# The opening of a transformer layer: where buffers lie, when late tiles are transposed, and where bias tables are written

## The chip, the cores and the metric

The kernel runs on one core of a Trainium2 chip. A core has a matrix engine (TensorE, PE in the profile), a vector engine (VectorE, DVE), a scalar engine (ScalarE, ACT), a general engine (GpSimd, POOL) and a queue engine (SyncE, SP). Each runs its own list of instructions in order and waits at semaphores for the others. DMA transfers are issued from the lists of SP, ACT and POOL. TensorE reads from the on-chip memory SBUF and writes to the accumulation memory PSUM, which has eight banks. The metric is the device time of one execution in microseconds (us). An execution's own time is slightly longer than the span of its instructions.

## The reference: one encoder layer

The input x has 1024 tokens of 1024 numbers. Everything is float32.

```
h = swiglu(rmsnorm(x, ffn1_pre_g), w_gate, w_up, w_down)       # 1024 -> 2816 -> 1024
x = x + 0.5 * rmsnorm(h, ffn1_post_g)
qkv = rmsnorm(x, mix_pre_g) @ w_qkv                            # 16 heads of 64
o_na  = neighbourhood_attention(q, k, v of heads 0..7,  na_rel_bias)
o_dil = dilated_mixture_attention(q, k, v of heads 8..15, t5_rel_bias)
x = x + rmsnorm(concat(rmsnorm(o_na), rmsnorm(o_dil)) @ w_out, mix_post_g)
h = swiglu(rmsnorm(x, ffn2_pre_g), ...)                        # second FFN
x = x + 0.5 * rmsnorm(h, ffn2_post_g)
```

`rmsnorm(x, g)` is `x / sqrt(mean(x*x) + 1e-6) * g`, and `swiglu(x)` is `(silu(x @ w_gate) * (x @ w_up)) @ w_down`. The dilated heads add a bias that depends on the distance of two tokens: a table of 511 values a head, looked up from `t5_rel_bias`.

## The kernel before, in words

**Arithmetic.** A float32 product is made from three faster ones. Each operand is split into a rounded part hi (a cast on ACT) and the rest lo (a subtraction on DVE), and `mm3` (lines 315 to 317) adds hi*hi, hi*lo and lo*hi in PSUM. The large products use Strassen's scheme (in Winograd's form) on 2 x 2 blocks: seven block products, of operands A11, S2, S1, S4, A12, S3 and A22 with weights B11, T2, T1, B22, B21, T3 and T4. For the tokens, tiles 0 to 3 (of 128 tokens each) are the upper half and tiles 4 to 7 the lower half; the sums S1 to S4 need both.

**The first FFN's opening.** `layer` writes the order of the head out by hand (lines 1436 to 1548): there PE, DVE and ACT follow the program's order, afterwards only PE does, and a scheduler places the other engines' instructions. Input tiles x0 to x3 are loaded, squared and summed (`square`, a pass on ACT, or on DVE for half a tile), scaled by the reciprocal root and the gain (`scaled`, line 1480), transposed on TensorE (line 157) and split (lines 164 and 165) into the columns of A11 and A12. A copy of every transposed half (line 236) goes to DRAM (line 237), where the later half tiles find it again. The gain row is spread over the partitions by a matmul (line 302) and copied in two halves (line 303).

**Turns.** `PairGemm.ahead` works through the first nine blocks (`early` = 9) of gate and up weights: a block is A11 (12 matmuls) times the gate weights and, one step later (`late`), A12 times the same weights. After each block a planned turn runs: `F` queues squares and scaling of two late tiles (4 to 7), `L` loads two tiles, `U` puts the two transposes of one late tile behind the next matmuls (`put`, `one`, `left_half`, `right_half`; DVE lines 264 to 274). Each group of matmuls calls `c.step()` twice, which runs one queued sum and one queued transpose. `ready`, before the ninth block, empties these queues, closes the pool `xp` and opens the pool of the full weight blocks; its two 8 KB (per partition) buffers `wraw` are loaded on SP (`fetch`, lines 405 and 406). `begin` then makes the weight sums of block 0 (lines 500 to 502) and splits them (lines 411 and 412), each behind the last DVE or ACT instruction issued so far. Only then `run` can start with S2.

**Memory.** Pools are stacked from the two ends of SBUF; `xp` and the pool that follows it lie at the right end. Inside a pool each tag has its own place, in the order in which the tags are first used. A tile waits for all readers of older tiles that lie on its place. The tags of `xp` are x (4 buffers of 4 KB), xn (3 of 4 KB), pre (the gain, 4 KB), s and x1.

**Runs over 22 blocks.** `run` (line 525 on) does the five remaining products of each early block in 60 matmuls; each block's sums are made one block ahead, and a weight buffer is loaded again as soon as its last split is done. The q,k projection later uses the same class with 8 blocks, all early, and writes q and k to DRAM from POOL (lines 928 to 934).

**Bias tables.** `bias_steps` (line 810 on) prepares the attention's tables on POOL's queue during the first FFN's `run`. `table(i)` makes two tables of 8 x 511 values (matmul on line 834) and `toeplitz(i, q)` (line 843) copies one of them from DRAM to DRAM into 32 shifted rows a head of `gab`, 511 KB each, eight copies in all, in turns 5 to 8. The first attention head reads `gab` (line 1005) when q,k's turn 5 has come.

Of the kernel before, what the change touches and what calls it, by code (L numbers as in the profile page):

```python
# [19 lines left out]
P, T = 128, 512  # L20
# [148 lines left out]
class Operand:  # L169
# [51 lines left out]
    def one(self, t, later=None):  # L221
# [6 lines left out]
        if t < 4:  # L228
            if t not in self.raw:
                two = c.xp.tile([P, 2, 2, 4, P], F32, tag="s", name="raw", bufs=c.deep)  # L230
                self.raw[t], self.raw[t + 1] = two[:, 0], two[:, 1]
            raw, i = self.raw[t], 0 if b == A11 else 1
            ps = transpose_in(c, src, *[h[:, :, cols] for h in self.x[b]])

            def keep():
                c.nc.scalar.copy(raw[:, i], ps)
# [55 lines left out]
def spread_gain(c, g, tag, row, one):  # L292

    nc = c.nc
    t = c.xp.tile([P, D], F32, tag=tag, name="gain", bufs=1)
    nc.gpsimd.memset(one, 1.0)
    nc.sync.dma_start(row, g)
# [92 lines left out]
class PairGemm:  # L390
# [4 lines left out]
    def __init__(self, c, op, srcs, early, sink):  # L395
        self.c, self.op, self.srcs, self.early, self.sink = c, op, srcs, early, sink
        self.n, self.raw, self.w, self.kept, self.own = len(srcs), {}, {}, {}, None
# [17 lines left out]
    def mm(self, ps, w, i, a, go_on=False, cols=slice(0, T)):  # L415
        hi, lo = w
        xhi, xlo = self.op.x[a]
        for k in range(4):
# [32 lines left out]
    def ahead(self, begun=(), ready=None):  # L451
# [358 lines left out]
def bias_steps(c, rel, t5, onehot, lncount, cmask):  # L810
# [420 lines left out]
def layer(tc, a, out):  # L1231
    nc = tc.nc
    c = Ctx(tc)
    with ExitStack() as ctx:
# [77 lines left out]
        def ffn(which, op, prep, pg, get, turns, sums, more, post, pre, src, dst, begin=None, tables=()):  # L1312
# [7 lines left out]
            if begin:  # L1320
                left_pool(e)
                pg.start()
# [113 lines left out]
        with ExitStack() as order:  # L1436
# [9 lines left out]
            half = [slice(0, T), slice(T, D)]  # L1446
            xs = {t: c.xp.tile([P, D], F32, tag="x", name="x", bufs=4) for t in range(4)}
            xn = [c.xp.tile([P, D], F32, tag="xn", name="xn", bufs=c.xn) for _ in range(2)] + [xs[2], xs[3]]
            op0 = Operand(c, None, 0)
            op0.gain, *gains = spread_gain(c, a["ffn1_pre_g"], "pre", xn[0][:1], xn[1][:1, :P])  # L1450
            for t in range(2):
                for h, q in enumerate((nc.sync, nc.scalar)):
                    q.dma_start(xs[t][:, half[h]], x0[t][:, half[h]])

            def begin(pg):
# [7 lines left out]
                def junk():  # L1463
                    return c.xp.tile([P, D], F32, tag="s", name="junk", bufs=2)
# [75 lines left out]
                for b in range(3):  # L1540
                    if b:
# [3 lines left out]
                    (lo0, lo1, lo2)[b](1)  # L1545
                order.close()
# [5 lines left out]
                                    {0: [F(4, 5), L(6, 7)], 3: [F(6, 7), U(4)], 4: [U(5)], 6: [U(6)], 7: [U(7)]},  # L1552
# [60 lines left out]
            plan(8, {5: [lambda: queued(load_head)], 7: [lambda: queued(load_head), lambda: queued(first_bias),  # L1613
# [204 lines left out]
```

## Time and profile before

| | us |
|---|---|
| median of 3 runs (lowest, highest) | 1928.7 (1925.5, 1930.73) |
| the profiled execution's own time | 1927.12 |
| its span, first to last instruction | 1925.3 |
| PE busy | 1850.6 (96%) |
| DVE busy | 1328.0 (69%) |
| ACT busy | 832.9 (43%) |
| POOL busy | 321.4 (17%) |

A line of the timeline gives the start in us, the duration in us, the engine, the line of the kernel, the operation with output and input, their shape, the count, and in brackets how long the engine had been idle and whose result ended the idle time. SPq, ACTq and POOLq are the queues in which DMA transfers are issued. A busy PE is not necessarily a PE at full speed: the stretches also give the granted clock.

### The profile page before, as it was taken

Reading aid. Unit: us, or ns where it says so; the run is one execution under the profiler, and the core shown is the slowest. Engines: PE = TensorE matmul, PEld = TensorE weight load, DVE = VectorE, ACT = ScalarE, POOL = GpSimd, SP = SyncE. Lnnn points to the kernel's source line nnn. Section 1 sums busy time; section 2 is a strip of 40 time slices with the busy share of each in tenths; the row PEclk is TensorE's granted clock in tenths of the full one; section 3 lists DMA queues with packets and bytes.
Section 4 is the critical chain, followed back from the end, with each engine's and each line's share of the span. In section 5 each row is a group of like instructions: output and inputs, shape, how many; then the busy total and the mean of one; then the engine's idle time right before and its main releaser. Section 6 shows DMA issues by size and latency. Waiting matters only on the chain.

```text
span 1925.3 us, 25132 instructions
## 1 busy us (share of the span) xinstructions
PE 1850.6 (96%) x8904; PEld 1535.5 (80%) x8904; DVE 1328.0 (69%) x2233; ACT 832.9 (43%) x1491; POOL 321.4 (17%) x504
## 2 busy tenths in 40 slices
PE   7899999999999999999999998998999999999997
PEld 5687787888878878788799997776888888888886
DVE  5877767766565878658577765678788777654557
ACT  6522233333443547323588765455222333344332
POOL 2123211110112013122423100021111111110000
PEclk9899999999999999999999999999999999999999
DMA  7646556653987767746877431475456655476663
GB/s 257 216 155 214 181 208 237 239 210 124 329 315 235 256 209 261 252 129 225 292 234 246 166 135 59 150 278 192 158 192 239 214 194 208 159 263 223 197 230 134
DMA packets 169008, 404.95 MB, mean 210 GB/s; under 512 B 17761, under 2 KB 40193, under 8 KB 166834
## 3 DMA queue, kind: packets, MB, share of 16 engines
q1 hardware_dynamic: 121042, 242.66, 37.7%
q0 software_dynamic: 46832, 158.59, 22.7%
q10 hardware_dynamic: 1008, 2.10, 0.3%
q8 instruction: 70, 1.15, 0.2%
q14 instruction: 56, 0.46, 0.1%
HBM read 277.34 MB, written 130.99 MB: 212 GB/s over the span
## 4 chain that ended last, share of the span: by engine, by line
PE 72%; DVE 9%; DMA 8%; issue 5%; ACT 4%; POOL 1%; SPq 0%; DVEq 0%; POOLq 0%; ACTq 0%
PE mmp L315 14%; PE mmp L317 14%; PE mmp L316 14%; PE accp L316 7%; PE accp L317 7%; PE accp L315 7%; DMA wraw<-in_wu_dram 3%; PE po L1064 2%; PE ptp L974 2%; PE po L1176 2%; DMA tsv<-tr 1%; PE sp L1043 1%; DVE pw L672 1%; DVE wlo L412 1%; PE sp L1160 1%
## 5 line engine op out<-in xcount | busy, mean ns | idle before, releaser
L315 PE MATMUL mmp<-x,whi 128*128 128x512 f32 (+1 forms) x1464 | 582.0, 398 | 28.5 <-ACT whi L411 11.9
L317 PE MATMUL mmp<-x,wlo 128*128 128x512 f32 (+1 forms) x1464 | 578.0, 395 | 1.2 <-DVE wlo L412 1.2
L316 PE MATMUL mmp<-x,whi 128*128 128x512 f32 (+1 forms) x1464 | 576.5, 394 | 0.8 <-DVE x L165 0.7
L315 PEld LDWEIGHTS mmp<-x,whi 128*128 128x128 f32 x1464 | 278.6, 190 | 93.9 <-ACT whi L411 17.5
L317 PEld LDWEIGHTS mmp<-x,wlo 128*128 128x128 f32 x1464 | 278.2, 190 | 66.5 <-DVE wlo L412 3.8
L316 PEld LDWEIGHTS mmp<-x,whi 128*128 128x128 f32 x1464 | 278.7, 190 | 62.0 <-DVE x L165 1.6
L672 DVE TENSOR_TENSOR pw<-praw,pw 128x1024 fp32r<-128x1024 f32 (+1 forms) x181 | 203.1, 1164 | 117.5 <-ACT pw L671 116.5
L671 ACT CAST pw<-praw 128x1024 fp32r<-128x1024 f32 (+1 forms) x181 | 168.8, 982 | 211.4 <-PE accp L317 151.9
L411 ACT CAST whi<-wraw 128x1024 fp32r<-128x1024 f32 x129 | 135.6, 1051 | 247.4 <-PE mmp L316 216.7
L316 PE MATMUL accp<-pw 128*128 128x512 f32 x600 | 234.0, 390 | 4.3 <-DVE pw L672 4.1
L315 PE MATMUL accp<-pw 128*128 128x512 f32 x600 | 234.5, 391 | 0.0
L317 PE MATMUL accp<-pw 128*128 128x512 f32 x600 | 233.6, 389 | 0.0
L412 DVE TENSOR_TENSOR wlo<-wraw,whi 128x1024 fp32r<-128x1024 f32 x129 | 158.3, 1228 | 27.0 <-ACT whi L411 26.9
L316 PEld LDWEIGHTS accp<-pw 128*128 128x128 f32 x600 | 112.7, 188 | 29.4 <-DVE pw L672 6.2
L315 PEld LDWEIGHTS accp<-pw 128*128 128x128 f32 x600 | 112.6, 188 | 23.9 <-ACT pw L671 0.3
L317 PEld LDWEIGHTS accp<-pw 128*128 128x128 f32 x600 | 112.6, 188 | 23.2
L619 POOL DMA_DIRECT2D g<-sg x44 | 23.9, 544 | 442.8 <-DVE sg L612 252.8
L411 ACT CAST whi<-traw 128x512 fp32r<-128x512 f32 x52 | 32.3, 622 | 148.4 <-DVE traw L501 92.6
L573 DVE TENSOR_TENSOR c<-mmp,u 128x512 f32<-128x512 f32 x52 | 35.8, 689 | 76.2 <-PE mmp L317 76.2
L430 ACT COPY s<-mmp 128x512 f32<-128x512 f32 x52 | 30.5, 587 | 129.5 <-PE mmp L317 117.2
L500 DVE TENSOR_TENSOR wraw<-wraw 128x1024 f32<-128x1024 f32 x52 | 63.6, 1223 | 32.1 <-DMA wraw<-in_wu_dram 26.2
L383 DVE TENSOR_TENSOR tr<-tr 128x1024 f32<-128x1024 f32 x26 | 31.7, 1219 | 39.4 <-DMA tr<-in_wd_dram 22.0
(275 smaller groups left out, 2774.4 us busy)
## 6 DMA issues: line engine op xcount, KB each, us to landing
praw<-g SPq DMA_DIRECT2D x70, 512.0 KB, 5.4
wraw<-in_wg_dram SPq DMA_DIRECT2D x44, 512.0 KB, 4.1
wraw<-in_wu_dram SPq DMA_DIRECT2D x44, 512.0 KB, 6.6
tr<-in_wd_dram SPq DMA_DIRECT2D x44, 512.0 KB, 6.5
g<-sg POOLq DMA_DIRECT2D x88, 256.0 KB, 3.5
ts<-tr POOLq DMA_DIRECT2D x22, 1024.0 KB, 4.7
praw<-ts SPq DMA_DIRECT2D x88, 256.0 KB, 4.3
praw<-in_wd_dram SPq DMA_DIRECT2D x66, 256.0 KB, 5.1
```

The lines of the kernel that those rows point to most:

```text
L315: nc.tensor.matmul(out, ahi, bhi, start=start, stop=False, skip_group_check=go_on)
L316: nc.tensor.matmul(out, ahi, blo, start=False, stop=False, skip_group_check=go_on)
L317: nc.tensor.matmul(out, alo, bhi, start=False, stop=stop, skip_group_check=go_on)
L411: nc.scalar.copy(hi, raw)
L412: nc.vector.tensor_sub(lo, raw, hi.bitcast(F32))
L500: nc.vector.tensor_sub(r[:, 0:2], r[:, 1:3], r[:, 0:2])
L573: nc.vector.tensor_add(c21, d, u2)
L671: nc.scalar.copy(hi, raw[:, :m])
L672: nc.vector.tensor_sub(lo, raw[:, :m], hi.bitcast(F32))
L974: nc.tensor.transpose(ps[:, j, :], src[:, j * P:(j + 1) * P], c.ident)
L1064: nc.tensor.matmul(po[:, un * 2 + j], pt[:, 2 * j + t, :], rhs, start=t == 0, stop=t == 1)
L1176: nc.tensor.matmul(po[0][:, u], pt[0][:, j, :], vs[:, k0 + j, :], start=j == 0, stop=j == n - 1)
```

## The change

Five things are changed.

1. `xp`'s tags are first used in the order s, x1, xn, pre, x. The third weight block (`w2`) lies in a buffer of x1 instead of xn, and the gain's tile is made by the caller of `spread_gain`.
2. In the head, the first two weight blocks are loaded in halves, the first halves ahead of x2 and x3 in the program, the second halves behind. The copies of the gain move behind squares, and the copies of the transposed tiles 2 and 3 (`keeps`) behind the last 6 matmuls of block 1's first group, which in turn move behind these tiles' transposes.
3. For the inline case of `one` (tiles 0 to 3), ACT makes the cast and the copy at once, and DVE subtracts from the copy in SBUF instead of from PSUM.
4. `ready` comes one block sooner in the first FFN (`before` = 2), and the late tiles' steps `U` two turns sooner (one for `F(6, 7)`).
5. The eight `toeplitz` copies move from the first FFN to turns 0 to 3 of the q,k run, two a turn, each behind POOL's last instruction.

```diff
@@ Operand.one
-            ps = transpose_in(c, src, *[h[:, :, cols] for h in self.x[b]])
+            hi, lo = [h[:, :, cols] for h in self.x[b]]
 
             def keep():
                 c.nc.scalar.copy(raw[:, i], ps)
                 c.nc.gpsimd.dma_start(self.saved[t][:, i], raw[:, i].rearrange("p k x -> p (k x)"))
-            keep() if later is None else later.append(keep)
+            if later is None:
+                ps = transposed(c, src)
+                c.nc.scalar.copy(hi, ps)
+                keep()
+                c.nc.vector.tensor_sub(lo, raw[:, i], hi.bitcast(F32))
+            else:
+                ps = transpose_in(c, src, hi, lo)
+                later.append(keep)
@@ PairGemm.ahead
-            if ready and b == self.early - 1:
+            if ready and b == self.early - self.before:
                 ready()
@@ bias_steps
-        for q in range(4):
-            step(5 + 2 * i + q // 2, toeplitz, i, q)
...
+    c.toeplitz = [lambda i=i, q=q: c.behind(lambda: toeplitz(i, q), POOL) for i in range(2) for q in range(4)]
@@ layer, head
+            first_junk = [c.xp.tile([P, D], F32, tag="s", name="junk", bufs=2)]
+            w2 = c.xp.tile([P, D], F32, tag="x1", name="w2", bufs=2)
+            xn = [c.xp.tile([P, D], F32, tag="xn", name="xn", bufs=c.xn) for _ in range(2)]
+            gain = c.xp.tile([P, D], F32, tag="pre", name="gain", bufs=1)
             xs = {t: c.xp.tile([P, D], F32, tag="x", name="x", bufs=4) for t in range(4)}
...
             def begin(pg):
+                for b in range(2):
+                    pg.raw[b] = c.wg.tile([P, 2, T], F32, tag="g", name="graw")
+                pg.raw[2] = w2.rearrange("p (i x) -> p i x", i=2)
+                for b in range(2):
+                    nc.sync.dma_start(pg.raw[b][:, 0], pg.srcs[b][0][:, half[0]])
                 nc.scalar.dma_start(xs[2], x0[2])
                 nc.sync.dma_start(xs[3], x0[3])
-                w2 = c.xp.tile([P, D], F32, tag="xn", name="w2", bufs=c.xn)
-                pg.raw[2] = w2.rearrange("p (i x) -> p i x", i=2)
+                for b in range(2):
+                    nc.sync.dma_start(pg.raw[b][:, 1], pg.srcs[b][0][:, half[1]])
                 nc.sync.dma_start(w2, pg.srcs[2][0])
...
                 square(0)
-                gains[0]()
                 square(1, 0)
                 square(1, 1, xn[1][:, half[1]])
+                gains[0]()
...
-                for f in keeps:
-                    f()
+                while keeps:
+                    keeps.pop(0)()
                 acc, s1 = [pg.bank() for _ in range(3)], []
-                for b in range(2):
-                    pg.mm(acc[b], pg.w[b], 0, A11, cols=slice(0, 256))
+                pg.mm(acc[0], pg.w[0], 0, A11, cols=slice(0, 256))
+                pg.mm(acc[1], pg.w[1], 0, A11, cols=slice(0, 256), ks=range(2))
                 r1 = next(root)
                 scaled(r1, 0, 2, 3)
-                op0.one(2)
-                op0.one(3)
+                op0.one(2, keeps)
+                op0.one(3, keeps)
+                pg.mm(acc[1], pg.w[1], 0, A11, cols=slice(0, 256), ks=range(2, 4))
+                while keeps:
+                    keeps.pop(0)()
...
+                pg.before = 2
...
-                                    {0: [F(4, 5), L(6, 7)], 3: [F(6, 7), U(4)], 4: [U(5)], 6: [U(6)], 7: [U(7)]},
+                                    {0: [F(4, 5), L(6, 7)], 1: [U(4)], 2: [F(6, 7), U(5)], 4: [U(6)], 5: [U(7)]},
@@ layer, q,k run
-            plan(8, {5: [lambda: queued(load_head)], 7: [lambda: queued(load_head), lambda: queued(first_bias),
+            plan(8, {**{i: c.toeplitz[2 * i:2 * i + 2] for i in range(4)}, 5: [lambda: queued(load_head)], 7: [lambda: queued(load_head), lambda: queued(first_bias),
```

More of the change, by code (lines that the diff above doesn't have):

```diff
@@ L289, in rstd_by_sqrt, with spread_gain @@
     yield y
-def spread_gain(c, g, tag, row, one):
+def spread_gain(c, t, row, one):
     nc = c.nc
-    t = c.xp.tile([P, D], F32, tag=tag, name="gain", bufs=1)
-    nc.gpsimd.memset(one, 1.0)
-    nc.sync.dma_start(row, g)
     copies = []
@@ L413, in split, with mm @@
         return hi, lo
-    def mm(self, ps, w, i, a, go_on=False, cols=slice(0, T)):
+    def mm(self, ps, w, i, a, go_on=False, cols=slice(0, T), ks=range(4)):
         hi, lo = w
         xhi, xlo = self.op.x[a]
-        for k in range(4):
+        for k in ks:
             sl = slice(k * P, (k + 1) * P)
@@ L1446, in layer @@
             half = [slice(0, T), slice(T, D)]
+            first_junk = [c.xp.tile([P, D], F32, tag="s", name="junk", bufs=2)]
+            w2 = c.xp.tile([P, D], F32, tag="x1", name="w2", bufs=2)
+            xn = [c.xp.tile([P, D], F32, tag="xn", name="xn", bufs=c.xn) for _ in range(2)]
+            gain = c.xp.tile([P, D], F32, tag="pre", name="gain", bufs=1)
             xs = {t: c.xp.tile([P, D], F32, tag="x", name="x", bufs=4) for t in range(4)}
-            xn = [c.xp.tile([P, D], F32, tag="xn", name="xn", bufs=c.xn) for _ in range(2)] + [xs[2], xs[3]]
+            xn += [xs[2], xs[3]]
             op0 = Operand(c, None, 0)
-            op0.gain, *gains = spread_gain(c, a["ffn1_pre_g"], "pre", xn[0][:1], xn[1][:1, :P])
+            nc.gpsimd.memset(xn[1][:1, :P], 1.0)
             for t in range(2):
@@ L1463, in junk @@
                 def junk():
-                    return c.xp.tile([P, D], F32, tag="s", name="junk", bufs=2)
+                    return first_junk.pop() if first_junk else c.xp.tile([P, D], F32, tag="s", name="junk", bufs=2)
                 def square(t, h=None, to=None):
```

6 lines of the change are left out of this document (4 added, 2 removed).

## The prediction

> **What bounds the kernel now.** I read the page first: the span, and the chain of work that ended last.
>
> ```profile
> span 1925.3 us, 25132 instructions
> ...
> PE 72%; DVE 9%; DMA 8%; issue 5%; ACT 4%; POOL 1%; SPq 0%; DVEq 0%; POOLq 0%; ACTq 0%
> ```
>
> TensorE carries 72% of the chain; what can be won is its idle time. Next, busy time by stretch (PE, PEld, DVE, ACT, POOL, then granted clock, DMA share, GB/s), for the first FFN's opening:
>
> ```profile
> 60.00:80.00 20.00, 20.00 (x96) 16.29 (x95) 19.14 (x28) 13.82 (x24) 4.33 (x8) 1.00 0.35 128
> 80.00:100.00 20.00, 11.56 (x37) 8.46 (x36) 11.11 (x14) 3.73 (x5) 0.54 (x1) 0.74 0.81 288
> ```
>
> PE is full until 80, then half idle at a clock of 0.74. The PE timeline (start, duration, and in brackets the idle time before) gives the places:
>
> ```profile
> 21.16 0.38 PE L315 MATMUL mmp<-x,whi 128*128 128x256 f32 x1 [2.07 <-ACT x L164]
> 21.89 0.39 PE L316 MATMUL mmp<-x,whi 128*128 128x256 f32 x1 [0.34 <-DVE x L165]
> ...
> 33.04 0.49 PE L315 MATMUL mmp<-x,whi 128*128 128x512 f32 x1 [2.32 <-ACT x L164]
> 33.88 0.50 PE L316 MATMUL mmp<-x,whi 128*128 128x512 f32 x1 [0.34 <-DVE x L165]
> ...
> 80.65 0.39 PE L317 MATMUL mmp<-x,wlo 128*128 128x512 f32 x1
> 89.11 0.80 PE L315 MATMUL mmp<-x,whi 128*128 128x512 f32 x1 [8.07 <-ACT whi L411]
> ...
> 90.70 0.80 PE L317 MATMUL mmp<-x,wlo 128*128 128x512 f32 x1 [0.37 <-DVE wlo L412]
> ...
> 95.56 0.57 PE L316 MATMUL mmp<-x,whi 128*128 128x512 f32 x1
> 95.97 0.40 PE L317 MATMUL mmp<-x,wlo 128*128 128x512 f32 x1
> ```
>
> A 512-column matmul starts every 0.233 us when TensorE is warm (80.65 is followed by nothing, so its slot ends at 80.88). Between 80.88 and 95.97 only 14 matmuls start, worth 3.3 us: 11.8 us are lost, 8.4 idle and 3.4 to the slow clock. This gap is the largest single loss of the kernel. What ends it, in the queue waits, the SP and the DVE timelines:
>
> ```profile
> SPq L405 <- DVE x L264: 23.9, 1, 23.9
> ...
> 80.33 0.65 SPq L405 DMA_DIRECT2D wraw<-in_wg_dram  x1
> ...
> 60.49 2.47 DVE L206 SCALAR_TENSOR_TENSOR xn<-x,y,gain 128x1024 f32<-128x1024 f32 x2
> ...
> 86.24 1.22 DVE L500 TENSOR_TENSOR wraw<-wraw 128x1024 f32<-128x1024 f32 x1 [5.93 <-DMA wraw<-in_wu_dram]
> ```
>
> SP stood 23.9 us before the first full weight load, until the last DVE split of a late tile (L264): the load's buffer lies on memory that these splits read. The input rows themselves are dead after L206, at 63.
>
> **The change, part by part.** *Buffers and the earlier ready step.* The xp tags are now made in the order s, x1, xn, pre, x. Before, the load waited for readers of s and x1, the last tags made; so the last tag lies where the next pool begins, and that is now x (4 x 4 KB, as large as the two 8 KB weight buffers). The load then waits for L206, at 63 or sooner. The ready step runs one turn sooner (24 matmuls, 5.6 us), and SP's remaining early loads are out by 56.2. So the load of 5.9 us (80.33 to 86.24) lies under matmuls. What is late next is DVE: L500, the two subtractions behind it and two splits, 86.24 to 90.65, 4.4 us, put behind the split of the ninth block and before the last 12 matmuls. I leave 0.8 us of gap: gain 11.0. Bounds: 4 (ready data, but the chain from 86.24 to 89.11 and part of the clock loss stay) to 11.8.
>
> *Head.* Rows of ACT, DVE and POOL:
>
> ```profile
> 6.50 0.58 ACT L303 COPY gain<-gps 128x512 f32<-128x512 f32 x1 [1.03 <-PE gps L302]
> 6.98 0.63 ACT L150 ACTIVATE junk<-x 128x512 f32<-128x512 f32 x1
> ...
> 7.74 0.16 DVE L281 TENSOR_TENSOR v<-ss 128x2 f32<-128x2 f32 x1 [1.76 <-ACT junk L150]
> ...
> 9.23 1.41 DVE L1480 SCALAR_TENSOR_TENSOR xn<-x,y,gain 128x512 f32<-128x512 f32 x2
> ...
> 20.03 0.58 ACT L236 COPY raw<-trp 128x512 f32<-128x512 f32 x1 [0.76 <-DVE x L165]
> ...
> 23.39 1.20 POOL L1444 DMA_DIRECT2D x<-in_x_dram  x2
> ...
> 28.39 1.06 ACT L150 ACTIVATE xn<-x 128x1024 f32<-128x1024 f32 x1 [0.99 <-DMA x<-in_x_dram]
> ```
>
> The square of tile 1 stood behind the gain copy, which waited 1.03 for its matmul. Now it fills that wait: DVE starts at 6.3 instead of 7.74, ACT's root follows the copy at 7.0, the first scaling comes at 8.1 instead of 9.23: 1.1 us. SP now loads the first halves of two weight blocks, then x3, then their second halves and the third block, which go to casts after the first scaling; its two more issues, 0.36 each like the others, stand ahead only of these late halves. The third block's buffer is now one of x1's two; tile 5's saved half needs it only at that tile's second transpose, so I charge nothing (without that cover, one 5 us load). At 21.16 the two casts L164 were parted by the copy L236, which waited for DVE. Kept for later, both go back to back, and 6 of the 24 narrow matmuls (0.12 us each) wait behind the transposes as cover: L316 starts near 18.5, not 21.89, so 3.4 us are won to there, the 1.1 among them. The stall at 33.04 had ACT waiting for tile 4's rows (28.39) ahead of the last casts. Their load, 23.39, follows the scaling of tiles 0 and 1 and moves by the same 3.4; so this stall may stay whole (gain 3.4), or go with its 2.7 idle and some 1.7 of slow clock (7.8). L236 no longer waits for DVE, which speaks for the upper half; the scheduler, free to put the squares before the casts, for the lower. I take 6.
>
> *Late tiles two turns sooner.*
>
> ```profile
> 35.51 1.28 DVE L206 SCALAR_TENSOR_TENSOR xn<-x,y,gain 128x1024 f32<-128x1024 f32 x1
> ...
> 48.01 0.60 PE L157 MATMUL trp<-ident,xn 128*128 128x128 f32 x4
> ...
> 66.54 0.60 PE L157 MATMUL trp<-ident,xn 128*128 128x128 f32 x4
> ```
>
> PE keeps program order, so a transpose moved forward makes all matmuls behind it wait for its tile. Tile 4's moves from 48.01 to the middle of the second A12 group, 39.5 by matmul count, 33.5 with the head's 6. Its tile was ready at 36.8, and at 33.4 if it moves by 3.4: no stall, or up to 3.3 if it doesn't move. Tile 6's had 4.8 us in hand (L206's first half ends at 61.7); its norm moves one turn and its transposes two, so 5.6 us less: a stall of 0.8. I charge 1 in all, 0 to 9 as bounds (9: tile 6's rows keep their time but for the turn). In return DVE, 19.1 of 20 busy before the gap, does the splits earlier: what it did from 20 to 90.65, some 51 us, has to fit from about 16.5 to 76, 86%. It fits, with little in hand.
>
> The opening so gives 11.0 + 6 - 1 = 16, the next group starting at 76.7 where a warm one would have at 92.7; 4 + 3.4 - 3 = 4 as the floor, 19.6 as the ceiling.
>
> *Bias tables.* Eight DRAM copies leave turns 5 to 8 of the first FFN. POOL timeline, chain, and stretches:
>
> ```profile
> 181.35 1.21 POOL L843 DMA_DIRECT2D gab<-tab  x2
> ...
> 184.63 10.59 DMA wraw<-in_wu_dram
> ...
> 194.00:208.00 14.00, 11.24 (x44) 8.92 (x43) 9.57 (x13) 3.14 (x4) 4.56 (x8) 0.90 0.66 187
> 208.00:222.00 14.00, 12.99 (x56) 10.29 (x56) 11.47 (x16) 4.41 (x5) 5.21 (x9) 0.98 0.45 133
> 222.00:236.00 14.00, 14.00 (x62) 11.34 (x61) 8.63 (x12) 3.82 (x5) 1.08 (x2) 1.00 0.71 259
> ```
>
> Against 62 matmuls, 18 and 6 are missing: 24 x 0.23 = 5.5 us. The small row copies stay, so 3 to 5.5 can be won; I take 5. They arrive two a turn in turns 0 to 3 of the q,k stage, on POOL right behind the k stores and some 3 us ahead of SP's weight loads. That stage (stretch, SP, DVE, ACT, DVE):
>
> ```profile
> 862.00:876.00 14.00, 14.00 (x64) 11.51 (x63) 11.90 (x16) 6.32 (x8) 3.71 (x5) 1.00 0.67 208
> ...
> 852.38 0.55 SPq L405 DMA_DIRECT2D wraw<-in_wqk_dram  x1
> ...
> 858.88 1.23 DVE L500 TENSOR_TENSOR wraw<-wraw 128x1024 f32<-128x1024 f32 x1 [1.09 <-DMA wraw<-in_wqk_dram]
> ...
> 863.64 1.06 ACT L411 CAST whi<-wraw 128x1024 fp32r<-128x1024 f32 x1 [1.24 <-PE mmp L316]
> ...
> 864.74 1.21 DVE L412 TENSOR_TENSOR wlo<-wraw,whi 128x1024 fp32r<-128x1024 f32 x1
> ```
>
> PE is full, but the loop behind it closes in just one block: load 6.5 us (852.38 to 858.88), DVE 7.1 (858.88 to the end of L412 at 865.95), together 13.6, and 60 matmuls at 0.227 are 13.6. The slack stands once: L411 waited for PE's group at 863.64, two groups of 12 later (869.1) PE needs L412's result, done at 865.95: 3.1 us. So if each load is x later, four turns lose 4x - 3.1. DMA has 0.67 of its time taken; two copies add 1.02 MB to 2.8 MB a block, about 0.87. POOL has 10 of 14 us free for their 1.2. I take x = 1.4, since 0.87 is still short of full, and lose 2.5; bounds 0 (x up to 0.8) and 15.7 (x = 4.7, from 5.9 to the 10.59 above). Gain of the move: 2.5.
>
> A page speaks against this part: the Trainium skill, "DMA: Bandwidth & Descriptors", section on queues, rings and completion order, says that each DMA engine goes round between the queues by packet, so POOL's copies would take turns with SP's loads. The trace agrees (10.59 beside the copies, 5.9 without); by that rule x is nearer to the upper bound, and the third rival below is what it makes.
>
> *The split from SBUF.* Tiles 0 to 3 of the later operands also get both ACT copies ahead of the DVE subtraction, the same 24 instructions. It matters where PE waited for L236:
>
> ```profile
> 1265.50 0.50 PE L315 MATMUL mmp<-x,whi 128*128 128x512 f32 x1 [3.47 <-ACT raw L236]
> ```
>
> There the copy stood behind two weight casts for DVE's sake; the first cast is needed as well, so 0.5 of 3.47 goes (0 to 1.5).
>
> **Sum.** 16 + 2.5 + 0.5 = 19. The profiled execution took 1927.1, 1.6 below the median of 1928.7; 1928.7 - 19 = 1909.7, so 1910.
>
> **Rivals.** *Late tiles stall PE.* PE reaches the transposes before L206, the stalls come to 9 and the opening gives 7: 1919. For it: rows 6 and 7 hang on POOL and DVE order. Against: x4 gets its load into a quiet stretch. Short stalls cost more than themselves: between 194 and 208 the clock fell to 0.90 after one of 2.76 us. The Trainium skill, "TensorE: Matmul & The Clock Gate", the part on the HAM clock gate, lets the clock fall only after about 3.4 us idle; the trace disagrees, and by the page such stalls would cost just their length.
>
> *The load waits as before.* The tag order doesn't put x under the weights, or a DVE split is queued before L500: the gap shrinks only by the two turns' earlier work, 4 instead of 11: 1917.
>
> *The tables' copies delay the q,k loads fully.* x = 4.7, 15.7 lost instead of 2.5: 1923, no change.
>
> *Slower.* The q,k blocks become bound by DMA. 3.85 MB a block at the 187 GB/s of the stretch 194 to 208 take 20.6 us, 7.0 over 13.6, four times 28 instead of 2.5: 1935. It decides from about 189 GB/s down. Against it, 208 GB/s are moved there at 0.67 busy.
>
> **How the numbers follow.** Forecast with its parts near my values 0.55 (1903 to 1915); stalls 0.17; the load still waiting 0.10; delayed loads 0.10; slower 0.08. A measurement of this kernel can tell about 0.3%, 5.8 us, from no change: 1922.9 to 1934.5. The first three cases are faster; of the delayed loads half lies within the bound. Faster 0.87, same 0.05, slower 0.08. The range, 1901 to 1923, leaves the last two cases out.
>
> **What would show it.** Right: no PE idle over 2 us between 75 and 95 and a full clock there; the first L405 issued before 65 and not ended by L264; L316's second half near 18.5; 62 matmuls in each 14 us around 180 to 210; in the q,k stage DVE's wait at L500 near 2.5. Wrong: long waits of PE at L157 before 70 (late tiles), L405 still behind L264 (buffers), PE waits in four q,k blocks (tables).

## The result, and the profile after

The changed kernel takes 1929.99 us in the median of 12 runs (1926.19 to 1932.02), the kernel before 1928.76 in the median of 12 beside them. The ratio is 1.0002, 95% interval 0.9989 to 1.0015: no change. The forecast was 1910, clearly faster. The profiled execution took 1926.19, its span is 1924.4.

First the opening, by stretches (PE, PEld, DVE, ACT, POOL, clock, DMA share, GB/s), then SP's queue waits, and the timelines of SP and PE.

```profile
40.00:60.00 20.00, 15.14 (x67) 11.96 (x66) 18.60 (x36) 13.01 (x22) 4.03 (x8) 0.92 0.73 234
60.00:80.00 20.00, 20.00 (x86) 16.11 (x86) 16.03 (x23) 11.53 (x19) 3.24 (x6) 0.91 0.63 211
80.00:100.00 20.00, 20.00 (x88) 16.24 (x87) 12.50 (x16) 5.96 (x9) 1.62 (x3) 1.00 0.47 170
```

```profile
SPq L409 <- DVE xn L206: 4.8, 1, 4.8
```

```profile
59.08 0.64 SPq L409 DMA_DIRECT2D wraw<-in_wg_dram  x1
```

```profile
18.89 0.39 PE L320 MATMUL mmp<-x,whi 128*128 128x256 f32 x1 [0.34 <-DVE x L165]
29.01 0.51 PE L319 MATMUL mmp<-x,whi 128*128 128x512 f32 x1 [2.60 <-ACT x L240]
30.34 0.80 PE L320 MATMUL mmp<-x,whi 128*128 128x512 f32 x1 [0.82 <-DVE x L242]
57.96 1.09 PE L157 MATMUL trp<-ident,xn 128*128 128x128 f32 x4 [4.86 <-DVE xn L206]
```

(L319 to L321 are `mm3`, L409 the first half of a full weight load, L504 to L506 the weight sums, L415 and L416 their splits: four lines more than before.) The half-empty stretch from 80 to 100 is full, and the load starts at 59.08 after a wait for the scaling L206, as forecast. A new gap stands at 57.96: 4.86 us of waiting for tile 6's scaled rows, with a clock of 0.92 and 0.91 around it.

Then the q,k stage: five stretches, DVE's waits at the weight sums, and the issues of the loads (SP) and of the copies (POOL).

```profile
832.00:846.00 14.00, 14.00 (x63) 11.62 (x62) 8.79 (x11) 4.80 (x6) 4.59 (x7) 1.00 0.87 273
846.00:860.00 14.00, 12.75 (x56) 10.25 (x55) 10.19 (x14) 5.92 (x7) 4.87 (x7) 1.00 0.75 220
860.00:874.00 14.00, 12.18 (x54) 9.77 (x53) 10.96 (x15) 5.83 (x7) 4.13 (x6) 1.00 0.60 176
874.00:888.00 14.00, 10.73 (x48) 8.55 (x46) 7.24 (x11) 4.82 (x7) 3.43 (x5) 1.00 0.71 251
888.00:902.00 14.00, 13.56 (x53) 11.07 (x54) 9.28 (x14) 3.06 (x4) 2.87 (x4) 0.88 0.65 200
```

```profile
844.94 1.23 DVE L504 TENSOR_TENSOR wraw<-wraw 128x1024 f32<-128x1024 f32 x1 [2.52 <-DMA wraw<-in_wqk_dram]
863.00 1.23 DVE L504 TENSOR_TENSOR wraw<-wraw 128x1024 f32<-128x1024 f32 x1 [6.08 <-DMA wraw<-in_wqk_dram]
881.36 1.23 DVE L504 TENSOR_TENSOR wraw<-wraw 128x1024 f32<-128x1024 f32 x1 [6.76 <-DMA wraw<-in_wqk_dram]
894.84 1.23 DVE L504 TENSOR_TENSOR wraw<-wraw 128x1024 f32<-128x1024 f32 x1 [4.62 <-DMA wraw<-in_wqk_dram]
```

```profile
837.00 0.55 SPq L409 DMA_DIRECT2D wraw<-in_wqk_dram  x1
...
852.06 0.55 SPq L409 DMA_DIRECT2D wraw<-in_wqk_dram  x1
...
870.12 0.55 SPq L409 DMA_DIRECT2D wraw<-in_wqk_dram  x1
...
887.72 0.55 SPq L409 DMA_DIRECT2D wraw<-in_wqk_dram  x1
```

```profile
833.49 1.21 POOL L847 DMA_DIRECT2D gab<-tab  x2
...
850.13 1.19 POOL L847 DMA_DIRECT2D gab<-tab  x2
```

From issue to sums the four loads take 7.9, 10.9, 11.2 and 7.1 us (844.94 - 837.00 and so on), where the one quoted before took 6.5. DVE waited about 1 us a block before and waits up to 6.76 now; of the 63 matmuls that a stretch holds, 7, 9 and 15 are missing in the second, third and fourth.

Where the time went is read by pairing matmuls: both kernels issue the same matmuls in the same counts, so the n-th product written to the same kind of PSUM tile can be compared in start time. The table gives the start after minus the start before, negative when the row's kernel is ahead; the heading is the start in the trace of before. The rows below the first are experiments.

| kernel | 21.9 | 43.8 | 72.4 | 95.1 | 172 | 215 | 483 | 834 | 942 | 1265 |
|---|---|---|---|---|---|---|---|---|---|---|
| changed | -3.0 | -0.8 | 5.3 | -6.2 | -8.2 | -14.5 | -19.4 | -15.4 | -1.4 | -3.4 |
| tables_alone | -0.1 | -0.6 | -0.6 | -0.4 | -0.9 | -7.1 | -12.0 | -11.4 | 3.6 | 3.4 |
| tables_back | -2.9 | -0.4 | 5.7 | -5.8 | -7.8 | -10.8 | -11.3 | -10.2 | -10.3 | -12.9 |
| norm67_first | -1.3 | 0.7 | -0.8 | -11.5 | -13.5 | -19.8 | -24.7 | -22.1 | -8.2 | -10.1 |
| norm_back | -2.9 | -0.3 | -1.9 | -12.6 | -14.5 | -14.6 | -13.7 | -12.8 | -12.8 | -17.3 |
| copies_small | -3.1 | -0.9 | 5.1 | -6.4 | -8.4 | -7.5 | -8.0 | -4.3 | 0.8 | -4.1 |
| sp_copies | -1.9 | 0.2 | 5.2 | -6.3 | -8.1 | -12.9 | -17.7 | -13.1 | -0.2 | -4.4 |
| sp_copies_s | -2.6 | -0.3 | 4.6 | -6.9 | -8.9 | -15.0 | -19.8 | -14.8 | -14.0 | -15.7 |
| before_sp | 0.3 | 0.0 | 0.0 | -0.7 | -2.7 | -9.0 | -13.8 | -8.6 | -8.6 | -9.6 |
| norm_back_sp | -3.2 | -0.8 | -2.3 | -13.0 | -15.0 | -21.3 | -26.2 | -25.5 | -25.5 | -27.1 |

Two things have to be known to read the table. At 43.8 the kernels with part 4 have already done the 16 transposes of tiles 4 and 5, which the kernel before does from 48 to 57; TensorE takes 1.7 us for them, so their rows show 1.7 less lead there than like for like (the changed kernel is really 2.4 ahead). At 72.4 and later all have done the same transposes. And each row is one execution: it can lie some us from its kernel's median (changed 1926.19 against 1929.99, norm_sp 1924.29 against 1919.71).

The changed kernel is 19.4 us ahead when the first FFN's second product begins (483): about the sum of the forecast, reached halfway. It loses 4.0 up to 834 (in that product and the value stage) and 14.0 in the q,k stage (to 942).

### The profile page after: what moved, and what is told of

Read it like the earlier page. It is cut to its first block, busy times and chain, and to the rows that moved or that the text cites. A ratio compares the mean times of both kernels' runs of the same rounds, so it can differ in the third digit from the quotient of the medians.

```text
span 1924.4 us, 25155 instructions
## 1 busy us (share of the span) xinstructions
PE 1849.8 (96%) x8904; PEld 1536.0 (80%) x8904; DVE 1325.0 (69%) x2233; ACT 830.9 (43%) x1491; POOL 319.1 (17%) x504
## 4 chain that ended last, share of the span: by engine, by line
PE 43%; issue 33%; DMA 8%; DVE 8%; POOL 4%; ACT 3%; SPq 0%; POOLq 0%; DVEq 0%; ACTq 0%
PE mmp L319 7%; PE mmp L320 7%; PE mmp L321 7%; PE accp L320 4%; PE accp L321 4%; PE accp L319 4%; PE po L1067 2%; PE ptp L977 2%; PE po L1179 2%; DMA wraw<-in_wqk_dram 2%; POOL g L642 1%; DMA tsv<-tr 1%; PE sp L1046 1%; PE sp L1163 1%; DVE pw L676 1%
## 5 line engine op out<-in xcount | busy, mean ns | idle before, releaser
L319 PE MATMUL mmp<-x,whi 128*128 128x512 f32 (+1 forms) x1464 | 581.1, 397 | 20.3 <-DVE v L550 9.2
L321 PE MATMUL mmp<-x,wlo 128*128 128x512 f32 (+1 forms) x1464 | 577.1, 394 | 2.3 <-DVE wlo L416 2.3
L320 PE MATMUL mmp<-x,whi 128*128 128x512 f32 (+1 forms) x1464 | 575.9, 393 | 1.3 <-DVE x L242 0.8
L319 PEld LDWEIGHTS mmp<-x,whi 128*128 128x128 f32 x1464 | 278.2, 190 | 85.0 <-ACT whi L415 10.4
L321 PEld LDWEIGHTS mmp<-x,wlo 128*128 128x128 f32 x1464 | 277.7, 190 | 66.7 <-DVE wlo L416 4.2
L320 PEld LDWEIGHTS mmp<-x,whi 128*128 128x128 f32 x1464 | 278.0, 190 | 62.6 <-DVE x L242 1.1
L676 DVE TENSOR_TENSOR pw<-praw,pw 128x1024 fp32r<-128x1024 f32 (+1 forms) x181 | 198.2, 1140 | 116.7 <-ACT pw L675 116.2
L320 PE MATMUL accp<-pw 128*128 128x512 f32 x600 | 234.1, 390 | 4.8 <-DVE pw L676 4.7
L415 ACT CAST whi<-wraw 128x1024 fp32r<-128x1024 f32 x129 | 135.3, 1051 | 232.9 <-PE mmp L320 201.4
L319 PE MATMUL accp<-pw 128*128 128x512 f32 x600 | 234.5, 391 | 0.8 <-DVE hb L732 0.8
L321 PE MATMUL accp<-pw 128*128 128x512 f32 x600 | 233.6, 389 | 0.0
L416 DVE TENSOR_TENSOR wlo<-wraw,whi 128x1024 fp32r<-128x1024 f32 x129 | 158.2, 1228 | 19.6 <-ACT whi L415 19.6
L320 PEld LDWEIGHTS accp<-pw 128*128 128x128 f32 x600 | 112.7, 188 | 30.3 <-DVE pw L676 7.3
L319 PEld LDWEIGHTS accp<-pw 128*128 128x128 f32 x600 | 112.6, 188 | 24.6 <-issue 1.2
L321 PEld LDWEIGHTS accp<-pw 128*128 128x128 f32 x600 | 112.6, 188 | 23.5
L415 ACT CAST whi<-traw 128x512 fp32r<-128x512 f32 x52 | 32.4, 622 | 145.7 <-DVE traw L505 90.3
L504 DVE TENSOR_TENSOR wraw<-wraw 128x1024 f32<-128x1024 f32 x52 | 63.7, 1224 | 39.7 <-DMA wraw<-in_wqk_dram 25.6
L1179 PE MATMUL po<-vs,pt 128*128 128x128 f32 x352 | 50.3, 276 | 2.0 <-ACT pt L979 1.7
```

Source lines behind the costliest of these rows:

```text
L319: nc.tensor.matmul(out, ahi, bhi, start=start, stop=False, skip_group_check=go_on)
L320: nc.tensor.matmul(out, ahi, blo, start=False, stop=False, skip_group_check=go_on)
L321: nc.tensor.matmul(out, alo, bhi, start=False, stop=stop, skip_group_check=go_on)
L415: nc.scalar.copy(hi, raw)
L416: nc.vector.tensor_sub(lo, raw, hi.bitcast(F32))
L504: nc.vector.tensor_sub(r[:, 0:2], r[:, 1:3], r[:, 0:2])
```

## The experiments

In the expectations of the first four, A is the theory that the moved copies cost the q,k stage what their removal wins, B its rival, that the rest of the change takes the time, and C that the norm of tiles 6 and 7 comes too late. Every time is a median, with the ratio to the kernel before, run beside it, and its 95% interval.

### The copies: back, alone, elsewhere

**tables_back**, the changed kernel with the copies left in the first FFN:

```diff
+        for q in range(4):
+            step(5 + 2 * i + q // 2, toeplitz, i, q)
...
-            plan(8, {**{i: c.toeplitz[2 * i:2 * i + 2] for i in range(4)}, 5: [lambda: queued(load_head)], ...
+            plan(8, {5: [lambda: queued(load_head)], ...
```

> The changed kernel with the eight table copies left in turns 5 to 8 of the first FFN, as in the kernel before; everything else as changed. Theory A (the copies in the q,k stage delay each weight load there and take back what the opening and the first FFN win): the five PE stalls of the q,k stage (1.3 to 3.7 us) go and about 13.9 us come back there, while 5.5 to 7.5 us are lost again in the first FFN: 1922 to 1924. Theory B (the q,k stage is slower for another reason, such as another order of DVE's work or the inline split, and the copies cost the predicted 2.5 or less): the q,k stalls stay, the first FFN loses 5.5 to 7.5 and the time is 1933 to 1937.

1917.35 us, ratio 0.9948 (0.9935 to 0.9962): faster than both theories had it, but it is A's case. It keeps through q,k what it has at 483 (-11.3, then -10.3).

**tables_alone**, the kernel before with nothing but that move, the same lines the other way round:

> The kernel before with nothing but the move of the eight table copies to turns 0 to 3 of the q,k stage. Theory A: the first FFN wins 5.5 to 7.5 and the q,k stage loses about 14: 1935 to 1937, with stalls of PE in the q,k stage after each pair of copies. Theory B: the q,k stage loses 2.5 at most: 1923 to 1926.

1932.7 us, ratio 1.0027 (1.0015 to 1.004). The time lies between the two ranges, since the first FFN wins more than expected: 12.0. q,k then loses 15.0, where B allows 2.5. So the move alone makes the whole round trip; B is out.

**tables_quiet**, the changed kernel with the copies one by one in the last value passes, when DMA has little to do:

```diff
-            vp.run(4, 5)
+            vp.run(4)
+            plan(8, {i: [c.toeplitz[i]] for i in range(8)})
+            vp.run(5)
```

> The changed kernel with the eight table copies put one by one into the last two passes of the value projection, just ahead of the q,k run, where DMA moved 90 GB/s at 0.29 busy. Theory A: the q,k stalls go and the first FFN keeps its gain; the copies cost 0 to 3 where they now are: 1915 to 1919. Theory B: as the changed kernel, 1928 to 1931.

1919.9 us, ratio 0.9968 (0.9954 to 0.9983). q,k still loses 8.1 (from 14.9 ahead at 834 to 6.8 at 942), in two steps. First, the copies were not out of the stage: its first matmul starts at 818.82, the last two copies are issued at 819.84 and 823.20. The small loads `s` beside them land in 6.3 us (median of three) instead of the 2.8 of before; DVE waits for one, TensorE 1.74 at 828.88, and 2.0 of the 8.1 are lost.

```profile
825.49 0.69 DVE L542 TENSOR_TENSOR u<-mmp,s 128x512 f32<-128x512 f32 x1 [5.77 <-DMA s<-s1d]
```

The other 6.2 go at one place, where no load is late. The scheduler has placed q,k's casts and stores otherwise: ACT's cast of k stands behind a store of an earlier block, and TensorE waits.

```profile
873.90 1.10 ACT L925 CAST qk<-k 128x512 fp32r<-128x512 f32 x1 [3.04 <-DMA qk<-qk]
```

```profile
887.89 0.57 PE L319 MATMUL mmp<-x,whi 128*128 128x512 f32 x1 [4.30 <-DVE v L550]
```

So there are two prices to a moved transfer: what it delays, and how the free engines' order changes with it.

**copies_small**, the changed kernel with the full copies in the first FFN and, at the four places in q,k, copies of the first 64 of each row's 511 values (the same values again, so nothing is left out):

```diff
+    def small(i, q):
...
+                      ap=[[1281, n], [P * 1280, 8], [1, 64]])
+        nc.gpsimd.dma_start(dst, tab[i, :, :64].unsqueeze(0).broadcast_to([n, 8, 64]))
```

> The changed kernel with the full copies left in the first FFN and repeated at the four places of the q,k stage with 64 of the 511 columns: as many issues on POOL at the same places, an eighth of the bytes. If it is the bytes that delay the weight loads: DVE's waits there fall to about 1 us and the time is that of the copies left in the first FFN, 1917 to 1920. If the issues themselves or the order they bring about cost the 14 us: 1928 to 1931.

1926.23 us, ratio 0.9979 (0.9965 to 0.9993): neither expectation. q,k loses 5.1, not 14.0 and not about 0. Issues with count, size and median time to landing in a stretch of 60 us or more of the q,k stage, first of the changed kernel, then of copies_small, then of tables_back:

```profile
wraw<-in_wqk_dram SPq DMA_DIRECT2D x8, 512.0 KB, 7.3
gab<-tab POOLq DMA_DIRECT2D x8, 511.0 KB, 7.4
```

```profile
wraw<-in_wqk_dram SPq DMA_DIRECT2D x8, 512.0 KB, 7.1
gab<-tab POOLq DMA_DIRECT2D x8, 64.0 KB, 6.6
```

```profile
wraw<-in_wqk_dram SPq DMA_DIRECT2D x10, 512.0 KB, 4.4
```

A copy with an eighth of the bytes takes 6.6 us instead of 7.4, and the median half-load behind it lands in 7.1 instead of 7.3; without copies it is 4.4. So a good part of the delay is not bytes. The worst loads are better (DVE waits 1.86, 3.59, 2.95 and 4.14).

### The copies on SP's queue

**sp_copies**, the changed kernel with the full copies in the same q,k blocks, issued on SP right behind a block's two loads:

```diff
@@ fetch
             nc.sync.dma_start(r[:, 1:3, :], up)
+            for f in self.extra.pop(b, ()):
+                c.behind(f, SP)
@@ toeplitz
-        nc.gpsimd.dma_start(dst, ...
+        nc.sync.dma_start(dst, ...
@@ layer, q,k run
+            pg.extra = {3 + i: c.toeplitz[2 * i:2 * i + 2] for i in range(4)}
```

> The changed kernel with the same eight full copies in the same q,k blocks, but issued on SP's queue right behind the two weight loads of a block, not on POOL's ahead of them. If the copies cost the q,k stage by taking turns with loads that are already due, and by the order of ACT and DVE that comes of it, the loads take some 6 us again and most of the 14 us is kept: 1915 to 1919. If the stage lacks the bandwidth for the copies, or SP's next loads now come too late behind them: 1926 to 1931.

1927.19 us, ratio 0.9992 (0.9977 to 1.0007): the rival's time, for its second reason. The weight loads are on time (DVE's longest wait for one is 0.94), TensorE loses nothing up to 883, and then two other waits come:

```profile
886.95 0.47 PE L319 MATMUL mmp<-x,whi 128*128 128x512 f32 x1 [3.59 <-DVE v L552]
920.61 0.77 PE L319 MATMUL mmp<-x,whi 128*128 128x512 f32 x1 [6.17 <-DVE v L552]
```

The first costs 3.9 us of lead, the second 8.7. The second hangs on a small load `s` on SP. SP issues it, at 910.17, behind loads for the attention, three of which take SP 7.74:

```profile
901.47 7.74 SPq L999 DMA_DIRECT2D va<-v  x3
909.25 0.87 SPq L1010 DMA_DIRECT2D g<-gab  x1
910.17 1.14 SPq L540 DMA_DIRECT2D s<-s1d  x2
```

```profile
918.57 0.69 DVE L544 TENSOR_TENSOR u<-mmp,s 128x512 f32<-128x512 f32 x1 [6.84 <-DMA s<-s1d]
```

**norm_sp**, the same with the early norm (below):

> The same, with the norm of tiles 6 and 7 queued ahead of tile 4's sums as well: if both repairs add up, 6 us below the run before, 1909 to 1913, the fastest of all. Rival: what the opening wins is lost again at the weight loads of the first FFN, as it was with the copies left there (2.4 of 6 kept): 1913 to 1917.

1919.71 us, ratio 0.9964 (0.995 to 0.9977): 7.5 less, as the norm adds, but above the expected times since sp_copies itself was. q,k loses 14.1 here (18.0 ahead at 834, 3.9 at 942).

**sp_copies_s**, sp_copies with the loads `s` of this stage on ACT's queue:

```diff
-                nc.sync.dma_start(s1, self.kept[b])
+                (nc.scalar if self.by_act else nc.sync).dma_start(s1, self.kept[b])
```

> The changed kernel with the copies on SP's queue behind the weight loads of the q,k blocks, and the small loads of the stage (s, of 256 KB) moved from SP's queue to ACT's. In the run with the copies on SP alone the weight loads were on time up to 883, and TensorE then stood 3.59 and 6.17, the second behind such a small load that SP issued late. If SP's order behind the copies is all that is left of the loss, both waits go: 1914 to 1919. If the stage lacks bandwidth with the copies in it, other waits take their place: 1924 to 1929.

1912.06 us, ratio 0.9923 (0.991 to 0.9937), below the range of its theory. q,k loses 0.8, with all the copies' bytes in it:

```profile
846.00:860.00 14.00, 14.00 (x64) 11.58 (x63) 11.61 (x15) 6.60 (x8) 4.32 (x6) 1.00 0.86 292
860.00:874.00 14.00, 14.00 (x63) 11.55 (x62) 10.87 (x15) 6.00 (x7) 3.89 (x6) 1.00 0.88 303
```

TensorE is full while DMA is 0.88 busy and moves 303 GB/s, more than in the stretches where the changed kernel starved. So it was not bandwidth that the stage lacked.

**before_sp**, the kernel before with its copies left in the first FFN but on SP, two each behind the loads of blocks 8 to 11:

> The kernel before with one thing altered: the eight copies of the first FFN on SP's queue, two each behind the weight loads of blocks 8 to 11, with every byte still in that stage. If the turns between the queues cost the 12 us that the removal of the copies won there: 1915 to 1920. If it was the bytes: 1926 to 1930.

1917.63 us, ratio 0.9949 (0.9937 to 0.9962). The first FFN wins 13.8, as much as without the copies. In the same stretch as the one quoted before (11.24 busy, clock 0.90):

```profile
194.00:208.00 14.00, 14.00 (x63) 11.50 (x62) 10.87 (x14) 4.50 (x6) 0.00 (x0) 1.00 0.49 171
```

It loses 5.2 of that between 483 and 834.

### The opening: the norm of tiles 6 and 7, the head

In the changed kernel the squares of tile 7, the last needed, end on ACT at 40.92, and DVE starts their root (L133) only at 49.51 and the scaling at 56.53:

```profile
40.73 0.19 ACT L150 ACTIVATION_READ_ACCUMULATOR xn<-x 128x1 f32 x1
```

```profile
49.51 0.16 DVE L133 TENSOR_SCALAR v<-ss 128x2 f32<-128x2 f32 x1
...
56.53 2.48 DVE L206 SCALAR_TENSOR_TENSOR xn<-x,y,gain 128x1024 f32<-128x1024 f32 x2
```

`norm` only queues the scaling in `c.sums`, a first-in, first-out queue in which the sums of tiles 4 and 5 stand ahead, moved forward by the change. **norm67_first** puts it in front:

```diff
+            def G(*ts):
+                n = op0.squares(ts, [xs[t] for t in ts])
+                op0.scale(*n)
+                for _ in ts:
+                    c.sums.appendleft(c.sums.pop())
...
-            ... 2: [F(6, 7), U(5)], ...
+            ... 2: [lambda: G(6, 7), U(5)], ...
```

> The changed kernel with one thing moved: the reciprocal root and the scaling of tiles 6 and 7 are queued in front of the waiting sums of tile 4 instead of behind them; their loads, squares and transposes stay where they are. Theory C (the stall of 4.9 us at tile 6's transpose, and the slow clock after it, come from DVE's queue: the norm stands behind the splits of tiles 4 and 5, which the change moved forward): the stall shrinks by at least 3 us, the slow clock after it goes, and 5 to 8 us are won: 1922 to 1925. Theory D (the rows of tile 7 arrive too late for any order): the stall stays within 1 us, 1929 to 1931.

1923.36 us, ratio 0.9979 (0.9966 to 0.9993).

```profile
42.63 0.17 DVE L133 TENSOR_SCALAR v<-ss 128x2 f32<-128x2 f32 x1
...
52.35 2.48 DVE L206 SCALAR_TENSOR_TENSOR xn<-x,y,gain 128x1024 f32<-128x1024 f32 x2
```

The root comes 6.9 us earlier, the scaling 4.2, and TensorE has no wait at tile 6. At 72.4 the lead is 6.1 better, and 6.7 at 834.

**norm_back**, norm67_first with the copies left in the first FFN:

> The changed kernel with two things altered: the copies stay in the first FFN, and the root and scaling of tiles 6 and 7 go ahead of tile 4's sums. If the two losses are independent, the 12.6 us and the 6.6 us add up: 1929.99 - 19.2 = 1911 (1908 to 1914). Rival: with the copies in the first FFN something else ends that stage, and the earlier norm is worth nothing there: 1917.

1914.98 us, ratio 0.9926 (0.991 to 0.9942): 2.4 below tables_back in the medians, 4.2 by the ratios (the kernel before took 1929.6 beside this one and 1926.9 beside tables_back). That alone doesn't exclude 6; the traces do, with a lead that is 7.6 better than tables_back's at 72.4 and 2.4 better at 483. The opening's 14.5 (at 172) do not grow by 215, where the kernels without copies on POOL's queue in that stage win 4.8 to 6.3 (tables_back 3.0).

**head_back**, norm_back with the head's loads, squares and copies in their old order (the head's lines of the change undone, buffers kept):

> The kernel of the run before (copies in the first FFN, norm of tiles 6 and 7 early), with the head's loads, squares and copies in their old order. Prediction's term: the head is worth 6, so 6 us slower than that run, 1917. Rival, read from the changed kernel's trace (4.0 us ahead at 29, 0.75 ahead at 43): the third stall and its slow clock give the gain back, so 0 to 2 us slower, 1911 to 1913.

1916.17 us, ratio 0.9937 (0.9918 to 0.9955): the head is worth 1.2 in the medians, the rival's case but within the scatter of the runs, and 2.4 at 43.8 (2.1 behind against 0.3 ahead).

**squares_behind**, norm_back with the squares of tiles 4 and 5 behind ACT's last instruction:

```diff
+            def F45():
+                n = []
+                c.behind(lambda: n.extend(op0.squares((4, 5), [xs[4], xs[5]])), ACT)
+                c.sums.append(lambda: op0.scale(*n))
```

> The same first kernel, with the squares of tiles 4 and 5 placed behind ACT's last instruction, so that no cast of the head stands behind a square that waits for its rows. Theory: the third stall (2.60 and 0.82 idle, 3.3 lost with the slow clock after it) goes, the head keeps 3 to 6 us more: 1905 to 1908. Rival: the squares come later, tile 4's transposes reach PE before its scaled rows, and the stall only moves: 1910 to 1916.

1915.74 us, ratio 0.9929 (0.9911 to 0.9947), the rival's case. The waits for the casts shrink from 3.03 and 0.83 to 0.68 and 0.72, and a new one takes their place:

```profile
36.37 1.09 PE L157 MATMUL trp<-ident,xn 128*128 128x128 f32 x4 [3.23 <-DVE xn L206]
```

### The split, and the fastest kernel

**split_alone**, the kernel before with part 3 alone:

> The kernel before with the split from SBUF alone. Prediction's term: 0.5 faster (0 to 1.5), by TensorE's wait of 3.47 at 1265.50. Rival, from the value stage, where the changed kernel lost 4 us that nothing else there explains: 2 to 5 us slower.

1927.98 us, ratio 0.9998 (0.9985 to 1.001). It is 3.7 ahead at 483 and 0.3 at 834. At the wait that the forecast names it wins 1.7 (from 1.4 ahead at 1262 to 3.1 at 1275), and by 1350 it loses 2.5 in waits for casts and splits of weights. The changed kernel has the same there, in place of the 3.47 for the copy:

```profile
1262.13 0.50 PE L319 MATMUL mmp<-x,whi 128*128 128x512 f32 x1 [2.40 <-ACT whi L415]
1263.54 0.50 PE L321 MATMUL mmp<-x,wlo 128*128 128x512 f32 x1 [0.68 <-DVE wlo L416]
```

**norm_back_sp**, norm67_first with the copies left in the first FFN, on SP as in before_sp:

```diff
+                pg.extra = {8 + i: [lambda k=k: c.toeplitz[k]() for k in (2 * i, 2 * i + 1)] for i in range(4)}
```

> The copies left in the first FFN, but on SP's queue, two each behind the weight loads of blocks 8 to 11, and the norm early. If there too it is the turns between the queues that delay the loads, about 5 us below the same kernel with the copies on POOL's queue (1915.0): 1909 to 1911. If it is the bytes (a block's loads and copies together exceed what its time lets through), no gain: 1914 to 1917.

1903.72 us (1901.13 to 1907.2), ratio 0.9873 (0.9852 to 0.9894): the fastest of all, and below the expectation. Its lead of 26.2 at 483 is still 25.5 at 942; in the opening of the second FFN it falls, from 28.3 at 1300 to 23.0 at 1350.

**nbs_nosplit**, that kernel without part 3 (`transpose_in` and `keep()` for all tiles, as before):

> The fastest kernel so far (copies in the first FFN on SP's queue, norm early, 1903.7) without the split from SBUF. By the run of that part alone (nothing in sum, 3 us won before and in the first FFN, 3 lost in the value stage): the same within 2 us, 1902 to 1906. Rival: the win in the first FFN was the copies' timing and not the split's, the loss in the value stage is the split's own: 3 us faster, 1900 to 1902.

1909.34 us, ratio 0.9917 (0.9902 to 0.9932): 5.6 slower in the medians (the two were not run side by side, but the intervals lie apart), 2.9 at 483 and 2.0 between the two profiled executions. Neither expectation: in this kernel the split from SBUF wins.

## Why the prediction was wrong, point by point

- **Buffers and the earlier ready step, 11.0: right.** L409 is issued at 59.08, released by L206 and not by a split (now L271); no wait between 75 and 95, clock 1.00 from 80 on. From 72.4 to 95.1 the changed kernel wins 11.5, norm67_first 10.7.
- **Head, 6: mis-sized, 2.4** (the changed kernel at 43.8, like for like; head_back gives the same there and 1.2 in the medians). L320 at 18.89 (18.5 forecast) won 3.0. The lower end of the range let the stall of 33.04 stay whole and the 3.4 survive it. It did come 4.0 earlier, at 29.01, with tile 4's square 3.1 earlier (25.33 instead of 28.39). But the clock behind it was lower than behind the old one. Stretches of before, then of the changed kernel:

```profile
33.00:36.00 3.00, 2.62 (x7) 1.94 (x8) 2.76 (x11) 1.98 (x3) 1.60 (x4) 0.75 1.04 395
36.00:39.00 3.00, 3.00 (x10) 2.34 (x9) 1.50 (x3) 1.20 (x3) 0.88 (x2) 0.68 1.01 362
```

```profile
30.00:33.00 3.00, 2.66 (x6) 2.15 (x7) 2.79 (x9) 0.00 (x0) 2.41 (x5) 0.50 1.03 419
33.00:36.00 3.00, 3.00 (x8) 2.31 (x7) 0.82 (x2) 0.64 (x1) 0.00 (x0) 0.50 1.04 419
```

Six us at 0.50 lose 3.0, six at 0.75 and 0.68 lose 1.7; with 0.5 more of idle time at the second wait (0.82 against 0.34) this accounts for the lead's fall from 4.0 to 2.4. The forecast let the moved stall cost at most what the old one did, clock included; it cost 1.3 more in clock. Its upper end, the squares behind the casts, is no way out either: in squares_behind the wait moved to tile 4's transposes. By the Trainium skill, "TensorE: Matmul & The Clock Gate", the part on the HAM clock gate, a window of about 3.4 us of activity decides; neither wait, 2.60 and 0.82, is that long, their sum is, and these rows don't tell which counts. Another place of the changed kernel is plainer: one wait of 2.12, at 934.08, is followed by a clock of 0.50 from 934 to 937, so here less than 3.4 was enough.
- **Late tiles, -1: mis-sized, -7.7** (from 2.4 ahead at 43.8, like for like, to 5.3 behind at 72.4; 4.86 idle, nearly all the rest at a clock of 0.50 from 57 to 63). The step that failed is "its norm moves one turn". The turn moved, but the norm waits in a queue behind eight sums, which the same change moved ahead of it. TensorE was free for tile 6's transposes at 53.10, 13.4 earlier than before, and the scaling started only 4.0 earlier (56.53, not 60.49): against each other they moved 9.5, where the forecast had 5.6. In norm67_first the same stretch loses 0.2. The first rival had the stall, near its size, and half the reason: it was DVE's order, but not POOL's, since the squares were done 8.6 us before the root. The floor of the opening, 4, was too high as well: it charged 3 for these stalls, whose own bound was 9.
- **Tables leaving the first FFN, 5: mis-sized, 11.** From 172 to 483 tables_alone wins 11.1 and the changed kernel 11.2. Some 6 of it go by 215, a little above the bound of 5.5. 5 more go where TensorE had waited 3.08 at 306.81 (DVE's c, L565), a wait that was not in the sum and that is gone in tables_alone, before_sp and the changed kernel, all without copies on POOL in that stage. In the kernel before DVE stands 5.77 just ahead of that (at 301.92) for a load of the next product's weights, and in tables_alone it doesn't; why that load is late, so long behind the last copy (243.35), isn't shown.
- **Tables entering q,k, -2.5: mis-sized, -14.0.** The mechanism held: with x = 1.4, 4.4, 4.7 and 0.6 over the 6.5 us load, the form 4x - 3.1 gives 8.0, and the lead falls by 9.2 up to the matmul at 910 in the trace of before (from 15.4 to 6.2); the rest falls in the block after, where DVE waits 3.11 for one more load and, behind that, ACT for a store of q and k:

```profile
923.12 0.63 ACT L920 ACTIVATE qk<-c 128x512 f32<-128x512 f32 x1 [7.65 <-DMA qk<-qk]
934.08 0.77 PE L319 MATMUL mmp<-x,whi 128*128 128x512 f32 x1 [2.12 <-DVE v L550]
```

The failed step is the choice of x = 1.4 "since 0.87 is still short of full". (0.87 is also too low by its own figures: 0.67 times 3.82 / 2.8 MB is 0.91.) The share of busy DMA time says nothing on how late a transfer is when another queue's is ahead of it: sp_copies_s has the same share, loads of 5.2 us, and TensorE doesn't wait. The near row was the 10.59 beside the copies in the first FFN. That was the third rival, given 0.10.
- **The split, +0.5: right in its mechanism, mis-sized, and lost again.** The wait for the copy is gone: 3.47 became 2.40 and 0.68, 0.4 less idle. The slow clock behind it, 0.50 from 1267 to 1270 in the kernel before, is gone too, which the term left out: 1.9 are won there, above the bound of 1.5. The blocks behind take it back (from 2.1 ahead at 1262 to 1.8 at 1350). Alone part 3 makes no difference (ratio 0.9998); in the fastest kernel it is worth 2.0 to 5.6. Which order of the other engines makes this difference isn't shown.
- **Not in the sum: 4.0 lost between 483 and 834**, 3.3 of it from 700 on. split_alone loses 3.4 and before_sp, without the split, 5.2; nbs_nosplit and norm_back_sp lose 0.5 and 0.7. New in the changed kernel are two waits for splits of weights (`pw`), 1.52 at 699.12 and 1.40 at 787.12. The order that the scheduler finds differs from kernel to kernel; what brings these waits about stays open.

Ahead of q,k 16 + 5 = 21 were forecast, and 19.4 had come by 483. That the two are close is luck: the opening gave 2.4 - 7.7 + 11.5 = 6.2 instead of 16, the tables' move twice its 5, and 2.0 between 95 and 172 were in no term. The rivals were priced one at a time, as if only one could come; two came together, late tiles and delayed loads, and the second alone took 14.

## What to carry to other kernels

Before moving a transfer into a stage whose loop closes on a load, look at which queue it is on and what is due just behind it, not at the stage's DMA share: the same bytes cost 14 us ahead of the loads on POOL's queue and 0.8 behind them on SP's, once the small loads were on ACT's. Behind them, look in turn at what that queue issues next: a small load pushed back there cost 8.7 us. When a step is moved forward, follow the queue it is put into: its inputs can be ready and its turn still not come.

## What the runs showed of the hardware

A DRAM-to-DRAM copy of 256 rows from POOL's queue takes 6.6 us with 64 KB and 7.4 with 511 KB, and half-loads on SP's queue beside it land in 7.1 and 7.3 us instead of 4.4. With the copies on SP behind the loads, as in sp_copies_s, the loads take 5.2 and the copies 10.1:

```profile
wraw<-in_wqk_dram SPq DMA_DIRECT2D x10, 512.0 KB, 5.2
gab<-tab SPq DMA_DIRECT2D x8, 511.0 KB, 10.1
```

The Trainium skill, "DMA: Bandwidth & Descriptors", section on queues, rings and completion order, has a DMA engine go round between the queues by packet. These rows agree so far: a copy on another queue delays the load, and one on the load's own queue, behind it, hardly does. What the runs don't separate: the move to SP changed the place in time (behind the loads instead of 1 to 3.5 us ahead of them) and the engine that issues the copies, as well as the queue.
